# Seven half-depth products for the second MLP matrix, six unit starts moved ahead, and per-head decays in the SSD scan of a hybrid decoder layer

## The chip, the cores and the metric

The kernel runs on one core of a Trainium2 chip. The metric is the device time of one launch in microseconds (us). The kernel before takes 2730.93 us (median of three runs, 2730.6 to 2733.95).

A core has five engines, each with its own queue of instructions taken strictly in order: TensorE (PE; its weight loads are listed as PEld), VectorE (DVE), ScalarE (ACT), GpSimd (POOL) and SyncE (SP, which here only starts DMAs). PE writes into PSUM, eight banks of 128 x 512 float32. A DMA is started by a queue (SP, ACT or POOL) and lands later; what reads its data waits on a semaphore.

## The reference, cut to what matters

The layer maps 1024 tokens of width 1024 (16 meta tokens lead) to the same shape, in float32:

```
h    = rmsnorm(x);  proj = h @ w_in                    # one wide projection
y_a, y_b, y_c = GLA(proj), sliding-window attention(proj), SSD(proj)
x    = x + (g0*(y_a@Wa) + g1*(y_b@Wb) + g2*(y_c@Wc)) @ w_out
h2   = rmsnorm(x)
hid  = square(relu(h2 @ w_mlp_in))                     # 1024 -> 4096
x    = x + hid @ w_mlp_out                             # 4096 -> 1024
out  = rmsnorm(x, final_norm)
# SSD, per head, in chunks of 128 positions:
seg[l,s] = a_cs[l] - a_cs[s];  L = exp(seg) for s <= l, else 0
y = ((C B^T) * L) @ (x*dt) + (C @ S_prev) * exp(a_cs) + D*x
```

## The kernel before, in words

Precision: a float32 operand is split into a high part (a cast to the reduced type `float32r`, on ACT) and a low part (the difference, on DVE). A product is the sum of three matmuls, high x high, high x low and low x high, summed in one PSUM bank. `w_split` and `w_cols` (L118 to L149) make the parts `w_hi` (L127) and `w_lo` (L128) of weights in tiles of 128 x 2048, two of each; `o_split` (L151 to L153) makes those of activations.

The work goes through these stages: normalisation and transposes, the GLA heads, the window attention, four SSD groups (`ssd`, L557), the three branch products with their gates (`branch`), the output projection (`wout`), and the MLP.

SSD scan (L628 to L673, at raised priority): a group has eight chunks. A chunk loads `ab`, the decay sums of its eight heads copied to all partitions (L632, 512 KB, two buffers); POOL subtracts the row's own sum (L635), DVE clips at zero (L636), ACT takes the exponential (L637), DVE multiplies by C B^T (L638), and PE forms eight 64-wide products with it (L643). PE then does C times the state (L646) and the state's update (L657). The sum `y` is gated, normalised (ACT, L664 and L666) and transposed on PE (L669) for the store. Between these steps PE works on "fillers": columns of the projection that do not depend on the scan (`zgen`, `ggen`), which end in L186 to L188 and L158 to L160.

First MLP product (L899 to L1032): a scheme of seven products instead of eight for 2 x 2 blocks (tokens in two halves, depth in two halves). Its activation operands `X` are 28 tiles (`x11`, `x21`, `x22`, `t1` to `t4`), made from transposed `h2` by DVE and ACT just before (L1002 to L1024). The weights come in 16 units of 256 columns; a unit makes four sums on DVE (L913 to L916) and seven operand pairs (L924, L925), and does seven products of 12 matmuls (`prod`, L929 to L937; the matmuls are L933, L935 and L936). Products share PSUM banks by accumulating. Results go through relu and square and to DRAM (`hid_out`, L939).

Second MLP product (L1034 to L1080): sixteen plain blocks of depth 256. A block loads its hidden rows and weights, splits them, and does 16 products of six matmuls of 128 x 512 (`tm2`, L843 to L849); each is added to the result tile `x2b` by DVE (L1062). The last block also does the final normalisation per token tile.

What sets the order: the kernel is written in program order, and a scheduler that models the engines' times at build time lays out one fixed list per engine, with raised priority for the SSD scan. Pools of buffers decide when a load may start.

Of the kernel before, what the change touches and what calls it, by code (L numbers as in the profile page):

```python
# [16 lines left out]
P = 128  # L17
D = 1024
# [26 lines left out]
def hybrid_layer_kernel(ctx, tc, x, meta_tokens, norm_mix, w_in, b_gate, gla_w_gate_up, gla_b_gate_up,  # L45
# [67 lines left out]
    hid_d = [dram.tile([P, SEQ], F32, name=f"hid{i}") for i in range(32)]  # L113

# [3 lines left out]
    def w_split(loads, cols, scales=None):  # L118
        hi = wp.tile([P, 2048], F32R, tag="whi", name="w_hi")
        lo = wp.tile([P, 2048], F32R, tag="wlo", name="w_lo")  # L120
        h = cols // 2
        for i in range(2):
            raw = raw_tile()
            loads(raw[:, :h], i)
            c = slice(i * h, (i + 1) * h)
            if scales is None:
                nc.scalar.copy(hi[:, c], raw[:, :h])  # L127
                nc.vector.tensor_tensor(lo[:, c], raw[:, :h], hi[:, c].bitcast(F32), sub)  # L128
                continue
            n = cols // len(scales)  # L130
            for k in range(h // n):
                sc, rc, c = scales[i * (h // n) + k], slice(k * n, (k + 1) * n), slice(i * h + k * n, i * h + (k + 1) * n)
                nc.scalar.activation(hi[:, c], raw[:, rc], AF.Copy, scale=sc)
                nc.vector.scalar_tensor_tensor(out=lo[:, c], in0=raw[:, rc], scalar=sc, in1=hi[:, c].bitcast(F32),
                                               op0=mult, op1=sub)
        return hi, lo

    def w_cols(view, ranges, scales=None):
        tot = sum(n for _, n in ranges)

        def loads(raw, i):
            rv = raw.rearrange("p (k c) -> p k c", k=KD // 2)
            o = 0
            for c, n in ranges:
                nc.sync.dma_start(rv[:, :, o:o + n], view[:, i * (KD // 2):(i + 1) * (KD // 2), c:c + n])
                o += n
        hi, lo = w_split(loads, KD * tot, scales)
        return (hi[:, :KD * tot].rearrange("p (k c) -> p k c", k=KD),
                lo[:, :KD * tot].rearrange("p (k c) -> p k c", k=KD))  # L149
# [16 lines left out]
    with p1:  # L166
# [390 lines left out]
        def ssd(g):  # L557
# [68 lines left out]
            if g < 3:  # L626
                zfill(8 * FZ[g], g + 1)
            with tc.high_priority(offset=HPE):  # L628
                for c in range(NT):
# [5 lines left out]
                    nc.gpsimd.tensor_tensor(ab, ab, up(tms[:, c, 32 + 8 * g:40 + 8 * g], 2, [P, 8, P]), sub)  # L635
                    nc.vector.tensor_scalar(ab, ab, 0.0, None, op0=amin)  # L636
# [5 lines left out]
                    for h in range(8):  # L642
                        nc.tensor.matmul(psD[:, h * 64:(h + 1) * 64], lhsT=ab[:, h, :], rhs=xd[:, h * 64:(h + 1) * 64],  # L643
                                         start=True, stop=True)
# [22 lines left out]
                    ps = bank(bk, "tr", 2)  # L667
# [444 lines left out]
```

## Time and profile before

| | us |
|---|---|
| median of three runs | 2730.93 |
| the profiled execution, whole | 2735.99 |
| its span in the profile | 2734.4 |
| PE busy in the span | 2634.5 (96%) |
| DVE busy | 1451.0 (53%) |
| ACT busy | 1049.2 (38%) |
| POOL busy | 386.2 (14%) |

The profiled execution is 5.06 us above the median of the runs; 1.59 us of it lie outside the span. Matmuls are pipelined, so their durations overlap: what one costs in a stream is the distance between two starts, not its listed duration. "Idle before" is the time that an engine waited ahead of an instruction and what ended it. The granted clock (PEclk) is a share of TensorE's full speed; it has two levels, 2.4 GHz (1.00) and 1.2 GHz (0.50), and a stretch shows the mean.

### The profile page before, as it was taken

What the parts mean: (1) busy time and instruction counts of PE and PEld (TensorE: products, weight loads), DVE (VectorE), ACT (ScalarE), POOL (GpSimd) and SP (SyncE); (2) the same over time, 40 slices, a digit from 0 to 9 for tenths busy, and PEclk for the clock granted to TensorE, in tenths of its full rate; (3) what the DMA queues carried; (4) which work ended last, traced back from release to release, by engine and by line L of the source; (5) the groups of instructions that cost most, each with busy time, mean ns of one, the idle gap of its engine ahead of it and who ended that gap; (6) DMA issues with size and microseconds to landing.
All of it is one profiled execution on the core that took longest, in us unless ns stands there. A gap on an engine that the chain in (4) does not pass through costs nothing.

```text
span 2734.4 us, 36866 instructions
## 1 busy us (share of the span) xinstructions
PE 2634.5 (96%) x14565; PEld 2284.4 (84%) x14565; DVE 1451.0 (53%) x2463; ACT 1049.2 (38%) x1915; POOL 386.2 (14%) x326
## 2 busy tenths in 40 slices
PE   8999999999999989989989899999998999999998
PEld 7998988888888979879879678888996888888887
DVE  5333323256664573653655653444437666676666
ACT  6423433246664454353454343323234333321212
POOL 1000000011221150340340410322200000000001
PEclk9999999999999999989989999999998999999999
DMA  4211112212223152252251464433322333533231
GB/s 141 63 40 54 47 47 62 77 52 76 61 68 93 51 123 74 67 122 74 76 133 46 122 224 150 150 113 110 124 78 81 108 108 113 204 124 96 93 100 62
DMA packets 223951, 260.48 MB, mean 95 GB/s; under 512 B 14382, under 2 KB 176484, under 8 KB 223780
## 3 DMA queue, kind: packets, MB, share of 16 engines
q1 hardware_dynamic: 178820, 207.74, 25.7%
q10 hardware_dynamic: 44960, 50.40, 5.2%
q8 instruction: 114, 1.87, 0.3%
q14 instruction: 57, 0.47, 0.1%
HBM read 195.05 MB, written 63.05 MB: 94 GB/s over the span
## 4 chain that ended last, share of the span: by engine, by line
PE 80%; DVE 5%; DMA 5%; ACT 4%; issue 3%; POOL 2%; SPq 0%; ACTq 0%; POOLq 0%; DVEq 0%
PE acc_ps L158 8%; PE acc_ps L159 8%; PE acc_ps L160 8%; PE pp_ps L778 8%; PE pp_ps L849 5%; PE pp_ps L847 5%; PE pp_ps L848 5%; PE pp_ps L781 4%; DMA ab<-acs_d 4%; PE pp_ps L933 3%; PE pp_ps L935 3%; PE pp_ps L936 3%; PE acc_ps L186 3%; PE acc_ps L188 3%; PE acc_ps L187 3%
## 5 line engine op out<-in xcount | busy, mean ns | idle before, releaser
L158 PE MATMUL acc_ps<-hh,w_hi 128*128 128x512 f32 (+6 forms) x1320 | 472.0, 358 | 3.3 <-ACT rt L352 1.7
L159 PE MATMUL acc_ps<-hl,w_hi 128*128 128x512 f32 (+6 forms) x1320 | 475.1, 360 | 0.0
L160 PE MATMUL acc_ps<-hh,w_lo 128*128 128x512 f32 (+6 forms) x1320 | 470.6, 356 | 0.0
L186 PE MATMUL acc_ps<-w_hi,hh 128*128 128x256 f32 x1056 | 308.4, 292 | 1.9 <-ACT zst L199 1.3
L187 PE MATMUL acc_ps<-w_lo,hh 128*128 128x256 f32 x1056 | 309.0, 293 | 0.0
L188 PE MATMUL acc_ps<-w_hi,hl 128*128 128x256 f32 x1056 | 308.1, 293 | 0.0
L128 DVE TENSOR_TENSOR w_lo<-w_raw,w_hi 128x1024 fp32r<-128x1024 f32 (+1 forms) x156 | 200.5, 1307 | 155.4 <-ACT w_hi L127 155.3
L158 PEld LDWEIGHTS acc_ps<-hh,w_hi 128*128 128x128 f32 (+1 forms) x1320 | 247.6, 188 | 32.8 <-ACT rt L352 2.6
L847 PE MATMUL pp_ps<-w_hi,o 128*128 128x512 f32 (+1 forms) x768 | 270.7, 354 | 1.4 <-ACT w_hi L127 1.4
L849 PE MATMUL pp_ps<-w_hi,o 128*128 128x512 f32 (+1 forms) x768 | 271.5, 354 | 0.1
L848 PE MATMUL pp_ps<-w_lo,o 128*128 128x512 f32 (+1 forms) x768 | 271.4, 354 | 0.0
L159 PEld LDWEIGHTS acc_ps<-hl,w_hi 128*128 128x128 f32 (+1 forms) x1320 | 247.8, 188 | 26.6 <-issue 2.4
L160 PEld LDWEIGHTS acc_ps<-hh,w_lo 128*128 128x128 f32 (+1 forms) x1320 | 248.0, 188 | 26.0 <-issue 2.4
L127 ACT CAST w_hi<-w_raw 128x1024 fp32r<-128x1024 f32 (+1 forms) x156 | 154.7, 1040 | 274.7 <-PE pp_ps L849 122.2
L188 PEld LDWEIGHTS acc_ps<-w_hi,hl 128*128 128x128 f32 x1056 | 201.3, 191 | 11.2 <-issue 10.5
L186 PEld LDWEIGHTS acc_ps<-w_hi,hh 128*128 128x128 f32 x1056 | 201.6, 191 | 9.2 <-issue 4.7
L187 PEld LDWEIGHTS acc_ps<-w_lo,hh 128*128 128x128 f32 x1056 | 201.3, 191 | 5.3 <-issue 4.4
L781 PE MATMUL pp_ps<-o,w_hi 128*128 128x512 f32 x512 | 198.9, 389 | 0.0
L778 PE MATMUL pp_ps<-o,w_hi 128*128 128x512 f32 x512 | 197.1, 389 | 1.2 <-ACT o L152 1.2
L1062 DVE TENSOR_TENSOR x2b<-pp_ps,x2b 128x512 f32<-128x512 f32 x256 | 169.3, 685 | 45.4 <-PE pp_ps L849 43.5
L933 PE MATMUL pp_ps<-o,w_hi 128*128 128x512 f32 x448 | 177.4, 398 | 9.3 <-ACT o L152 9.2
L935 PE MATMUL pp_ps<-o,w_hi 128*128 128x512 f32 x448 | 177.2, 395 | 2.1 <-DVE o L153 2.1
(298 smaller groups left out, 4657.1 us busy)
## 6 DMA issues: line engine op xcount, KB each, us to landing
w_raw<-in_w_in_dram SPq DMA_DIRECT2D x80, 512.0 KB, 3.7
ab<-acs_d SPq DMA_DIRECT2D x32, 512.0 KB, 9.2
g<-gate SPq DMA_DIRECT2D x64, 256.0 KB, 4.0
w_raw<-in_w_mlp_in_dram SPq DMA_DIRECT2D x32, 512.0 KB, 4.1
hid<-hid ACTq DMA_DIRECT2D x64, 256.0 KB, 3.3
w_raw<-hid SPq DMA_DIRECT2D x32, 512.0 KB, 4.4
w_raw<-in_w_mlp_out_dram SPq DMA_DIRECT2D x32, 512.0 KB
gate<-gst ACTq DMA_DIRECT2D x48, 256.0 KB, 2.0
```

Of the source, the lines that this page charges most:

```text
L158: nc.tensor.matmul(ps, lhsT=lh, rhs=rh, start=(i == 0), stop=False)
L159: nc.tensor.matmul(ps, lhsT=lh, rhs=rl, start=False, stop=False)
L160: nc.tensor.matmul(ps, lhsT=ll, rhs=rh, start=False, stop=(i == n - 1))
L186: nc.tensor.matmul(o, lhsT=h_h, rhs=whi[:, k, off:off + width], start=(k == 0), stop=False)
L187: nc.tensor.matmul(o, lhsT=h_h, rhs=wlo[:, k, off:off + width], start=False, stop=False)
L188: nc.tensor.matmul(o, lhsT=h_l, rhs=whi[:, k, off:off + width], start=False, stop=(k == KD - 1))
L778: nc.tensor.matmul(ps[b], lhsT=lh, rhs=xs[b][:, 0, :], start=(st and k == 0), stop=(sp_ and k == n - 1))
L781: nc.tensor.matmul(ps[b], lhsT=lh, rhs=xs[b][:, 1, :], start=False, stop=False)
L847: nc.tensor.matmul(ps, lhsT=x[:, 0], rhs=rh, start=(i == 0), stop=False)
L848: nc.tensor.matmul(ps, lhsT=x[:, 0], rhs=rl, start=False, stop=False)
L849: nc.tensor.matmul(ps, lhsT=x[:, 1], rhs=rh, start=False, stop=(i == n - 1))
L933: nc.tensor.matmul(ps, lhsT=h[:, kk, :], rhs=x[:, 0, :], start=(first and kk == 0), stop=False, skip_group_check=True)
```

## The change

1. The second MLP product is done in seven half-depth products too. The hidden units are taken in four groups (`q`) of eight units; a group does seven products, each 4 token tiles x 4 depth steps x 3 matmuls of 128 x 512. The activation operands (`x11`, `x21`, `x22`, `t1` to `t4`) are written by the first product's units: `t1` to `t4` are sums that POOL forms there, so a unit now stores seven tiles where it stored four. The weight operands `s1` to `s4` are sums that POOL forms in place. Results are added to tiles of `x2b` and to a fourth set `rr`, which the last group adds to three quarters of the result.
2. In the first MLP product each product has its own PSUM bank, and DVE combines them afterwards.
3. The products `x11` and `x21` of units 0 to 5 are done early, two units at a time, between the steps that make the operands (`pre`). Their intermediate result goes to DRAM and comes back by a DMA on POOL's queue; so does the finished `x11` tile.
4. In the SSD scan the subtraction and the clipping of the decays become eight DVE instructions, one for each head, with the head's sum as a per-partition scalar. The transposes of a chunk's `y` are issued after the next chunk's eight products.
5. Weight parts lie in tiles of 128 x 1024, four of each instead of two of double width; `final_norm` is loaded late; the final normalisation is done as the quarters of the last group finish.

The diff, cut to its core:

```diff
-        hi = wp.tile([P, 2048], F32R, tag="whi", name="w_hi")
-        lo = wp.tile([P, 2048], F32R, tag="wlo", name="w_lo")
+    def hilo():
+        return (wp.tile([P, 1024], F32R, tag="whi", name="w_hi", bufs=4),
+                wp.tile([P, 1024], F32R, tag="wlo", name="w_lo", bufs=4))
...
-                    nc.gpsimd.tensor_tensor(ab, ab, up(tms[:, c, 32 + 8 * g:40 + 8 * g], 2, [P, 8, P]), sub)
-                    nc.vector.tensor_scalar(ab, ab, 0.0, None, op0=amin)
+                    for h in range(8):
+                        nc.vector.tensor_scalar(ab[:, h, :], ab[:, h, :], tms[:, c, 32 + 8 * g + h:33 + 8 * g + h], 0.0,
+                                                op0=sub, op1=amin)
...
+                    if c:
+                        with tc.issue_after(mm.ins):
+                            y_out(c - 1, yn)
...
+        def pre(u):
+            ws_ = []
+            for i in range(2):
+                raw = raw_tile()
...
+                hi, lo = hilo()
+                nc.scalar.copy(hi, raw)
+                nc.vector.tensor_tensor(lo, raw, hi.bitcast(F32), sub)
...
+            for v in range(2):
+                w = [[t[:, :, v * P:(v + 1) * P] for t in pair] for pair in ws_]
+                a = ps_tile()
+                prod(a, w[0], "x11", True, True)
+                p1 = g_tile()
+                nc.scalar.copy(p1, a)
+                nc.scalar.dma_start(p1_d[u + v], p1)
+                unit_b(u + v, {"a": a, "w": {2: w[1]}})
...
+            if u < NPRE:
+                nc.gpsimd.dma_start(st["p1"], p1_d[u])
+                return
...
-            prod(st["b"], st["w"][7], "t3", False, True)
-            nc.vector.tensor_tensor(st["u3"], st["b"], st["p1"], sub)
+            b = ps_tile()
+            prod(b, st["w"][7], "t3", True, True)
+            nc.vector.tensor_tensor(st["u3"], b, st["u2"], add)
...
+            nc.gpsimd.tensor_tensor(t1, st["x11"], g, sub)
+            hid_out(u, "t1", t1)
+            nc.gpsimd.tensor_tensor(t2, st["x22"], t1, add)
+            hid_out(u, "t2", t2)
+            nc.gpsimd.tensor_tensor(t3, g, st["x22"], sub)
+            hid_out(u, "t3", t3)
+            nc.gpsimd.tensor_tensor(t4, st["x21"], t2, sub)
+            hid_out(u, "t4", t4)
...
-        NB = 16
-        for blk in range(NB):
...
+        def product(ps, xo, wo, first, last, done):
+            for t in range(4):
+                ts = slice(t * P, (t + 1) * P)
+                for kk in range(4):
+                    (xh, xl), (wh, wl) = xo[kk], wo[kk]
...
+                done(t, ps[t])
...
+        for q in range(NQ):
...
+            product(a, *o1, True, True, first_r)
+            product(a, *o2, False, True, evict("c11", add))
+            b = four()
+            product(b, x_op(q, "t3"), w_op(q, wr, "s3"), True, True, evict("c22", add))
+            a = four()
+            product(a, x_op(q, "t2"), w_op(q, wr, "s2"), True, True, evict("r", sub))
...
+            product(b, x_op(q, "t4"), w_op(q, wr, "a22"), False, True, c21_done)
+            c = four()
...
+            product(c, x_op(q, "t1"), w_op(q, wr, "s1"), True, True, c22_done)
+            product(c, x_op(q, "x22"), w_op(q, wr, "s4"), False, True, c12_done)
```

Three places in the engines' lists are shown. On PE, in a scan chunk before, the transposes of `y` (L669) stand ahead of the next chunk's eight products (L643), with filler matmuls (`acc_ps`) in front of them:

```order
L187 MATMUL acc_ps<-w_lo,hh_172 128x256
L188 MATMUL acc_ps<-w_hi,hl_180 128x256
L186 MATMUL acc_ps<-w_hi,hh_173 128x256
L669 MATMUL ps_tr<-ident,y 128x128 x4
L643 MATMUL ps_y<-xd,ab 128x64 x8
L646 MATMUL ps_y<-S,CF 128x512
L657 MATMUL ps_y<-xe,BT 128x512
L187 MATMUL acc_ps<-w_lo,hh_173 128x256
```

In the changed kernel the same eight products are L666, C times the state is L672, the state's update is L683 and the transposes are L644:

```order
L201 MATMUL acc_ps<-w_hi,hl_214 128x256
L666 MATMUL ps_y<-xd,ab 128x64 x8
L672 MATMUL ps_y<-S,CF 128x512
L199 MATMUL acc_ps<-w_hi,hh_199 128x256
L200 MATMUL acc_ps<-w_lo,hh_199 128x256
L201 MATMUL acc_ps<-w_hi,hl_207 128x256
L199 MATMUL acc_ps<-w_hi,hh_200 128x256
L644 MATMUL ps_tr<-ident,y 128x128 x4
L683 MATMUL ps_y<-xe,BT 128x512
```

The transposes of a chunk moved from ahead of the next chunk's products to behind them, beside the state matmuls.

On PE at the start of the MLP, before: the transposes of `h2` (L892) of the second token half with the matmuls of unit 0 (L933, L935, L936) between them:

```order
L892 MATMUL pp_ps<-ident,h_17706 128x128 x7
L892 MATMUL pp_ps<-ident,h_17715 128x128 x7
L933 MATMUL pp_ps<-o,w_hi 128x512
L892 MATMUL pp_ps<-ident,h_17724 128x128 x7
L935 MATMUL pp_ps<-o,w_hi 128x512
L936 MATMUL pp_ps<-o,w_lo 128x512
L933 MATMUL pp_ps<-o,w_hi 128x512
L935 MATMUL pp_ps<-o,w_hi 128x512
L936 MATMUL pp_ps<-o,w_lo 128x512
L892 MATMUL pp_ps<-ident,h_17733 128x128 x7
```

The same place now, where the matmuls L954, L956 and L957 belong to the early products of units 0 to 5 and L905 are the transposes:

```order
L905 MATMUL pp_ps<-ident,h_18066 128x128 x2
L905 MATMUL pp_ps<-ident,h_18075 128x128 x4
L905 MATMUL pp_ps<-ident,h_18084 128x128 x4
L954 MATMUL pp_ps<-o,w_hi 128x512 x4
L905 MATMUL pp_ps<-ident,h_18093 128x128 x4
L956 MATMUL pp_ps<-o,w_hi 128x512
L957 MATMUL pp_ps<-o,w_lo 128x512
L954 MATMUL pp_ps<-o,w_hi 128x512
L956 MATMUL pp_ps<-o,w_hi 128x512
L957 MATMUL pp_ps<-o,w_lo 128x512
```

From the first transpose of `h2` to the last matmul of the early products PE's list now holds 64 transposes and 180 matmuls of 512 columns; the early products are 144 of them.

On DVE in the second MLP product, before: additions to the result (L1062) with the low parts of the next block's weights (L128) and hidden rows (L153):

```order
L128 TENSOR_TENSOR w_lo<-w_raw,w_hi 128x1024
L1062 TENSOR_TENSOR x2b_20046<-pp_ps,x2b_20046 128x512
L1062 TENSOR_TENSOR x2b_20048<-pp_ps,x2b_20048 128x512 x2
L1062 TENSOR_TENSOR x2b_20050<-pp_ps,x2b_20050 128x512
L153 TENSOR_TENSOR o<-w_raw,o 128x512
L1062 TENSOR_TENSOR x2b_20050<-pp_ps,x2b_20050 128x512
L153 TENSOR_TENSOR o<-w_raw,o 128x512
L1062 TENSOR_TENSOR x2b_20052<-pp_ps,x2b_20052 128x512 x2
```

Now, with the additions at L1212, low parts of weights at L1192 and of hidden rows at L1161:

```order
L1212 TENSOR_TENSOR x2b_20704<-x2b_20704,pp_ps 128x512
L1192 TENSOR_TENSOR w_lo<-o,w_hi 128x1024
L1212 TENSOR_TENSOR x2b_20705<-x2b_20705,pp_ps 128x512
L1161 TENSOR_TENSOR o<-raw_21506,o 128x1024
L1192 TENSOR_TENSOR w_lo<-o,w_hi 128x1024
L1212 TENSOR_TENSOR o<-o,pp_ps 128x512 x3
L1161 TENSOR_TENSOR o<-raw_21512,o 128x1024
L1212 TENSOR_TENSOR o<-o,pp_ps 128x512
```

A product of 48 matmuls now has four additions and four low parts of 1024 columns around it; the low parts of later operands stand between the additions of the product that is running.

## Rows read from the trace of the kernel before

**Rows 1.** Page, part 1: busy time, share and instructions of each engine.
```profile
PE 2634.5 (96%) x14565; PEld 2284.4 (84%) x14565; DVE 1451.0 (53%) x2463; ACT 1049.2 (38%) x1915; POOL 386.2 (14%) x326
```

**Rows 2.** Busy time by stretch: us, each engine's busy time (count), PEclk, DMA share, GB/s.
```profile
103.00:500.00 397.00, 394.68 (x2597) 353.32 (x2596) 122.33 (x246) 136.65 (x255) 22.61 (x34) 1.00 0.16 49
850.00:1598.00 748.00, 693.92 (x4259) 627.43 (x4258) 421.13 (x585) 318.50 (x495) 200.72 (x152) 0.95 0.34 89
...
2037.55:2080.00 42.45, 28.36 (x114) 18.91 (x112) 36.79 (x63) 33.63 (x61) 5.07 (x4) 0.73 0.13 44
2080.00:2708.00 628.00, 626.64 (x2761) 518.62 (x2762) 415.25 (x633) 156.43 (x251) 0.09 (x1) 1.00 0.33 110
```

**Rows 3.** Busy time by stretch: the four SSD scans.
```profile
954.00:1038.00 84.00, 70.32 (x458) 60.39 (x457) 56.09 (x70) 43.88 (x63) 42.05 (x33) 0.92 0.51 122
1134.00:1225.00 91.00, 77.54 (x425) 63.09 (x424) 55.15 (x70) 39.37 (x58) 45.09 (x33) 0.87 0.49 112
1335.00:1420.00 85.00, 72.20 (x452) 61.26 (x451) 54.93 (x70) 43.39 (x62) 42.22 (x33) 0.88 0.51 121
1515.00:1597.00 82.00, 72.85 (x356) 55.41 (x355) 54.96 (x69) 29.92 (x49) 37.75 (x31) 0.96 0.41 113
```

**Rows 4.** Waits of PE, 850 to 1600 us: total us, times, longest.
```profile
PE ps_tr L669 <- ACT y L666: 39.3, 20, 4.9
PE ps_y L643 <- DVE ab L638: 11.0, 8, 2.7
```

**Rows 5.** Timeline: start, us, engine, line; three of PE's matmuls and 32 transposes.
```profile
2037.55 3.66 PE L892 MATMUL pp_ps<-ident,h 128*128 128x128 f32 x32
...
2695.74 0.39 PE L847 MATMUL pp_ps<-w_hi,o 128*128 128x512 f32 x1
...
2708.66 0.39 PE L847 MATMUL pp_ps<-w_hi,o 128*128 128x512 f32 x1
...
2724.08 0.39 PE L849 MATMUL pp_ps<-w_hi,o 128*128 128x512 f32 x1
```

**Rows 6.** DVE groups by form: count, busy us, mean ns, idle before and releaser.
```profile
L128 DVE TENSOR_TENSOR w_lo<-w_raw,w_hi 128x1024 fp32r<-128x1024 f32 x154 | 199.7, 1319 | 155.4 <-ACT w_hi L127 155.3
L1062 DVE TENSOR_TENSOR x2b<-pp_ps,x2b 128x512 f32<-128x512 f32 x256 | 169.3, 685 | 45.4 <-PE pp_ps L849 43.5 <-PE pp_ps L936 1.5
L638 DVE TENSOR_TENSOR ab<-ab,cb 128x1024 f32<-128x1024 f32 x32 | 43.3, 1363 | 13.0 <-ACT ab L637 13.0
L636 DVE TENSOR_SCALAR ab<-ab 128x1024 f32<-128x1024 f32 x32 | 35.6, 1112 | 85.1 <-POOL ab L635 85.1
L872 DVE TENSOR_SCALAR h<-x,rs 128x1024 f32<-128x1024 f32 x8 | 6.0, 750 | 2.5 <-POOL rs L88 2.5
L532 DVE TENSOR_SCALAR mxs<-mxs 128x4 f32<-128x4 f32 x32 | 7.6, 238 | 0.7
L86 DVE TENSOR_SCALAR ms<-yss 128x1 f32<-128x1 f32 x32 | 4.7, 148 | 15.1 <-ACT zt L664 14.9
```

**Rows 7.** ACT groups by form.
```profile
L127 ACT CAST w_hi<-w_raw 128x1024 fp32r<-128x1024 f32 x154 | 154.0, 1048 | 274.7 <-PE pp_ps L849 122.2 <-PE acc_ps L159 72.0 <-PE pp_ps L781 63.8
L924 ACT CAST w_hi<-mt 128x512 fp32r<-128x512 f32 x64 | 39.6, 622 | 102.9 <-PE pp_ps L935 57.4 <-DVE mt L913 45.0 <-DVE mt L914 0.4
L637 ACT ACTIVATE ab<-ab 128x1024 f32<-128x1024 f32 x32 | 33.8, 1057 | 42.6 <-DVE ab L636 42.5
```

**Rows 8.** POOL groups by form.
```profile
L635 POOL TENSOR_TENSOR ab<-ab,tms 128x1024 f32<-128x1024 f32 x32 | 63.4, 1980 | 139.9 <-DMA ab<-acs_d 127.6 <-PE acc_ps L188 8.5 <-PE ps_y L657 3.7
```

**Rows 9.** Timeline, 1835 to 1844 us: POOL additions and DVE side by side.
```profile
1835.70 5.43 POOL L817 TENSOR_TENSOR mg<-mg,g 128x512 f32<-128x512 f32 x4 [16.34 <-DVE g L816]
...
1837.49 5.90 DVE L134 SCALAR_TENSOR_TENSOR w_lo<-w_raw,vecs,w_hi 128x256 fp32r<-128x256 f32 x8
```

**Rows 10.** The line L134: shortest, median and longest duration in ns.
```profile
L134 DVE SCALAR_TENSOR_TENSOR w_lo<-w_raw,vecs,w_hi x64: 468/474/1519, 1750.5 to 1908.2; 128x256 fp32r<-128x256 f32 x64
```

**Rows 11.** Page, part 6: DMA issues, KB each, median us to landing.
```profile
ab<-acs_d SPq DMA_DIRECT2D x32, 512.0 KB, 9.2
g<-gate SPq DMA_DIRECT2D x64, 256.0 KB, 4.0
```

More of the change, by code (lines that the diff above doesn't have):

```diff
@@ L627, in ssd, with y_out @@
                 zfill(8 * FZ[g], g + 1)
+            def y_out(c, y):
+                ps = bank(bk, "tr", 2)
+                for i in range(4):
+                    nc.tensor.transpose(out=ps[:, i * P:(i + 1) * P], in_=y[:, i * P:(i + 1) * P], identity=ident)
+                st = ep.tile([P, CH], F32, tag="st", name="yst", bufs=2)
+                nc.scalar.copy(st, ps)
+                nc.scalar.dma_start(ossd[g].rearrange("(i p) t -> p i t", p=P)[:, :, c * P:(c + 1) * P],
+                                    st.rearrange("p (i t) -> p i t", i=4))
             with tc.high_priority(offset=HPE):
@@ L666, in ssd @@
                     nc.scalar.activation(y, y, AF.Copy, scale=rs)
[L667 to L673 removed]
+                    yn = y
+                y_out(NT - 1, yn)
         es = ExitStack()
@@ new lines, in hybrid_layer_kernel, with final, final_out @@
+        ys, sqs = {}, {}
+        def final(t, n):
+            if t not in sqs:
+                sqs[t] = sm.tile([P, 2], F32, tag="sq", name="sq", bufs=8)
+            y = tp.tile([P, 512], F32, tag="g", name="ysq", bufs=4)
+            nc.scalar.activation(y, x2[t][:, n * 512:(n + 1) * 512], AF.Square, accum_out=sqs[t][:, n:n + 1])
+        def final_out(t):
+            ss = sm.tile([P, 1], F32, tag="ss", name="ss3")
+            nc.vector.tensor_tensor(ss, sqs[t][:, 0:1], sqs[t][:, 1:2], add)
+            rs = rstd_of(ss, D, "rs3")
+            for n in range(2):
+                c = slice(n * 512, (n + 1) * 512)
+                y = x2[t][:, c]
+                if t < NT - 1 and n == 1:
+                    nc.scalar.activation(y, y, AF.Copy, scale=rs)
+                    nc.gpsimd.tensor_tensor(y, y, fnb[:, c], mult)
+                else:
+                    nc.vector.scalar_tensor_tensor(out=y, in0=y, scalar=rs, in1=fnb[:, c], op0=mult, op1=mult)
+                nc.sync.dma_start(out2d[t * P:(t + 1) * P, c], y)
@@ new lines, in hybrid_layer_kernel, with x_op @@
+        acc_c = {"c11": [], "c21": [], "c12": [], "c22": []}
+        for t in range(NT):
+            b = t // 4
+            acc_c["c12" if b else "c11"].append(x2[t][:, 0:512])
+            acc_c["c22" if b else "c21"].append(x2[t][:, 512:1024])
+        rr = []
+        for i in range(2):
+            t = hl_tile().bitcast(F32)
+            rr += [t[:, 0, :], t[:, 1, :]]
+        acc_c["r"] = rr
+        NQ, fnb = 4, None
+        def x_op(q, nm):
+            tiles = []
+            for i in range(2):
+                if q == 0 and nm in ("x11", "x21"):
+                    r = raw_tile().rearrange("p (v t) -> p v t", v=2)
+                else:
+                    r = tp.tile([P, 2, 512], F32, tag="h2", name="raw2", bufs=4)
+                nc.sync.dma_start(r, hid_d[2 * q + i, nm].rearrange("(v p) t -> p v t", p=P))
+                hi, lo = hl_tile(), hl_tile()
+                nc.scalar.copy(hi, r)
+                nc.vector.tensor_tensor(lo, r, hi.bitcast(F32), sub)
+                for v in range(2):
+                    tiles.append((hi[:, v, :], lo[:, v, :]))
+            return tiles
```

278 lines of the change are left out of this document (169 added, 109 removed).

## The prediction

> **What bounds the kernel now.** I began with the page's busy times [rows 1]: PE is busy for 96% of the span, so time goes only where PE gets less work or where it waits or runs slow today. The table by stretch says where that is [rows 2]. The GLA stretch is full (394.7 of 397 us), and so is the MLP from 2080 us (626.6 of 628, granted clock 1.00). Two places are not full. The SSD part has PE busy for 694 of 748 us, and the MLP's first 42 us have PE busy for 28, at a mean clock of 0.73. Third came the four scans [rows 3]: 342 us in all, PE busy for 293, so 49 us idle, with a clock of 0.87 to 0.96; the lost share of the clock times each length is another 32 us. The waits there [rows 4] say that PE stood 20 times in front of the transposes of `y` (39.3 us) and 8 times in front of the products with `ab` (11.0). The tail is fourth: the last matmul starts at 2724.08 [rows 5] and the span is 2734.4, so about 10 us are left for the last additions and the normalisation.
>
> **A. Second product, fewer matmuls.** Before: 16 blocks x 16 products x 6 = 1536 matmuls of 512 columns. Now: 4 groups x 7 products x 48 = 1344, so 192 are gone. In the full stretch one costs 626.64/2761 = 0.227 us [rows 2]; two starts 57 matmuls apart, 12.92 us [rows 5], say the same. PE sets the pace there, so 192 x 0.227 = **-43.6 us**. What has to be hidden beside a product of 48 x 0.227 = 10.9 us: DVE has four low parts of 1.32 and four additions of 0.685, 8.0 us [rows 6]; ACT four casts of 1.05, 4.2 us [rows 7]; POOL two sums of 1.98 [rows 8] in four of seven products. Each fits. Low parts rise from 64 to 112 of 1024 columns, additions to the result fall from 256 to 124, which for DVE is a gain of 27 us off the path.
>
> **B. Start of the MLP.** The stretch 2037.55 to 2080 holds 64 transposes at 3.66/32 = 0.114 us [rows 5] and 50 matmuls at 0.227: 18.7 us of work at full speed in 42.45, so 23.7 are lost to waits for operands and to the low clock. The list now holds 64 transposes and 180 matmuls there, 48.2 us. ACT has its 33.6 us [rows 2] and six casts of 1.05, and a net thirteen operations of 512 columns at 0.62 [rows 7]: 48 us. DVE has 36.8 and six low parts of 1.32 less two sums of 0.685: 43.3. PE and ACT are then level, so I take 52 us, 3.8 lost: **-19.9 us**. If nothing is lost it is -23.7; if the three engines hand work over as badly as today and the stretch takes 64 us, -8.
>
> **C. Units 0 to 5.** They now have five products left, 60 x 0.227 = 13.6 us. DVE has 18 operations of 512 columns (four sums, five low parts, nine combinations, each product now being its own bank) at 0.685 [rows 6]: 12.3 us. POOL adds beside it: four POOL additions of that size, 5.43 us, ran beside eight DVE operations that took 5.90 [rows 9], where a median one of them takes 0.474 [rows 10], so 3.8: 2.1 us more. That makes 14.4 against 13.6, 0.8 x 6 = 5 us. The new waits add to it. The twelve reloads of `p1` and `x11` are started from POOL's queue, behind its additions; DVE's subtraction waits for `p1` with all later combinations queued behind it, and POOL's `t1` waits for `x11`, with three more sums and the next reload behind it. A load half as large lands 4.0 us after its issue, and at the worst 9.2 [rows 11]; a unit lasts 14, so most are early, and I put 3 us for six units. **+8 us**, from 0 to 25. In units 6 to 15 DVE has 20 x 0.685 + 2.1 = 15.8 against 84 x 0.227 = 19.1: hidden.
>
> **D, E, F. Smaller terms.** The second product's first operands become free only as the last unit ends, and `x2b` is loaded again: **+4** (0 to 12, the far end being one landing [rows 11] and one cast and low part). Steady contention of POOL's sums with DVE over 28 products: **+3** (0 to 20, the far end by rival 3). The tail: the normalisation now starts as quarters finish, about two fewer DVE passes at the end: **-2** (-4 to +2).
>
> The finer weight tiles of edit 5 have the same count and size of casts; GLA, where most of them are, is full: 0 (-3 to +3). The MLP's sum is -50.5, from -73 to -24.
>
> **G. The scans.** A scan's chunk takes 342/32 = 10.7 us. Its `ab` has two buffers, so one loop of load, use and release may take two periods. Before, the loop is: landing 9.2 [rows 11], POOL's subtraction 1.98 [rows 8], clip 1.11, exponential 1.06 [rows 7], multiplication 1.36 [rows 6], and 16 PE starts at the 0.114 of [rows 5], 1.9: 16.6 us, with hand-overs about 18, that is 8.9 us a chunk at least. POOL's idle time before L635 ends mostly on that load (127.6 of 139.9 us) [rows 8], so POOL itself is not what is late. Now POOL's step is gone, and the clip becomes eight operations of 128 columns. No such form is in the trace; it lies between 0.148 for one column and 0.238 for four, which is a small operation's fixed part, and 0.750 for 1024 columns [rows 6]. I take 0.19, 1.5 us for eight; the far end 0.238, 1.9 us. The loop shrinks by 1.98 - 0.4 = 1.6 to 1.7, 0.85 a chunk, 27 us over 32 chunks if the loop sets the pace. To it I add 9 us, a quarter of the 39.3 that PE stood in front of the transposes [rows 4]: behind the products they no longer hold back the next chunk, but the state's update L683 and the fillers still stand behind them. **-36 us.** The two ends: PE's own work in the scans at full clock is 293 less the clock's part, about 265, 8.3 a chunk; if that sets the pace at 8.4, the gain is 2.3 x 32 = 73. If DVE sets the pace (221/32 = 6.9 us a chunk now [rows 3]) and the eight operations cost 0.238 each, 0.8 x 32 = 25 us are added.
>
> **The sum.** -43.6 - 19.9 + 8 + 4 + 3 - 2 - 36 = -86.5. The profiled execution is 2735.99 us (a span of 2734.4 and 1.59 around it), so a like execution takes 2649.5. The median of the runs is 5.06 below the profiled one, which gives 2644.4, said as **2645 us**.
>
> **Rivals.**
> 1. The scans gain nothing: the load of `ab` sets their pace and DVE's extra work eats POOL's step. For it: the 127.6 us [rows 8]. Against it: the step does leave the loop. 2645 + 36 = 2681.
> 2. The scans become PE's, and the MLP has no new stalls: 37 us more there, and 13 of C, D and E not paid. For it: PE's 39.3 us of waits in its own queue [rows 4]. 2595.
> 3. POOL's additions hold DVE for their whole time. For units 0 to 5 DVE then has 12.3 + 5.43 = 17.8 against 13.6, 4.2 x 6 = 25 us; in the 16 products with sums 8.0 + 3.96 = 12.0 against 10.9, 18 us. Against 8 us allowed for these two, 35 more: 2680. For it: DVE's eight operations stretched beside POOL [rows 9]; against it: by 2.1 us and not by 5.43.
>
> The Trainium skill bears on this rival (SBUF — State Buffer, "SBUF: two separate sides"): DVE, in an operation with two SBUF inputs, and GpSimd hold a shared pair of ports as an exclusive lock for a whole instruction, and the other "fully blocks". By that rule the time is rival 3's; the trace agrees in the direction and shows 2.1 of 5.43 us.
>
> 4. Slower than before: the second product's operands are late at each of its 28 products. There are four weight tiles of each part, two products' worth. From a freed tile to the next operand stand two casts of 1.05, two low parts and two splits of hidden rows of 1.32, and four additions of 0.685 queued between them, 10.1 us in 10.9. With POOL's two sums in the same chain it is 14.1, 3.2 late, and with 0.3 for hand-overs 3.5 x 28 = 98 us: 2743. It decides from 86/28 = 3.1 us late per product. Against it: only 16 products have such sums, they can be formed ahead, and a landing of 4 to 9 us is ahead of the tile.
>
> That the change doesn't do what it says I leave out: the engines' lists show the transposes behind the products, and 144 early matmuls.
>
> **How the numbers follow.** Forecast 0.57, own range 2612 to 2680 (the ends of B to F and a third of G's); rival 1 0.14, rival 2 0.12, rival 3 0.12, rival 4 0.05. The range of 8 in 10 is 2600 to 2695: it takes in rivals 1 and 3, both with some ten us on top, and leaves out rival 4 and about half of rival 2. A measurement of this kernel tells 0.2%, some 5.5 us, from no change. Only rival 4 ends above: slower 0.05, the same 0.02 (from its edge), faster 0.93.
>
> **What would show it.** A: 1344 matmuls at 0.227 us in the second product, PE gapless; an average above 0.24 is E or rival 4, and PE's waits would name L1192 or POOL's L1183. B: from the first transpose of `h2` to the last early product some 52 us, clock near 1. C: 14.5 us a unit, waits at the subtraction of `p1`. G: scans near 76 us instead of 85, the wait of the transposes on `y` mostly gone, DVE's eight operations under 0.2 us each; 85 us again is rival 1, 67 rival 2. Rival 3: DVE's 512-column operations lasting over 1 us beside POOL. It is wrong altogether if PE is idle for over 80 us in the second product.

## The result and the profile after

The changed kernel takes 2697.99 us, median of four runs (2695.72 to 2701.56), beside 2730.76 us for the kernel before on the same chip: a ratio of 0.9879, 95% interval 0.9862 to 0.9896. The forecast was 2645 us with a range up to 2695. The profiled execution took 2697.15 us with a span of 2695.5. The spans differ by 38.9 us and the medians by 32.8, since the profiled execution of before lay 5 us above its median and this one did not.

Busy times of the changed kernel [rows 1], page, part 1:

```profile
PE 2612.5 (97%) x14373; PEld 2245.8 (83%) x14373; DVE 1502.5 (56%) x2577; ACT 1096.4 (41%) x1930; POOL 513.9 (19%) x402
```

Its stretches [rows 2] in the same columns (us, busy time and count of PE, PEld, DVE, ACT, POOL, then PEclk, DMA share, GB/s). In order: GLA, the SSD stage from 850 us to the first branch matmul, the branches, the start of the MLP to the last transpose of `h2`, a part of the first product, the start and the rest of the second:

```profile
103.00:500.00 397.00, 395.16 (x2594) 354.00 (x2594) 126.58 (x249) 137.99 (x257) 22.60 (x34) 1.00 0.17 51
...
850.00:1591.30 741.30, 689.55 (x4228) 620.44 (x4226) 425.27 (x806) 322.35 (x497) 134.62 (x120) 0.95 0.34 90
1591.30:1949.00 357.70, 357.68 (x1534) 288.00 (x1535) 150.57 (x210) 121.30 (x213) 62.09 (x45) 1.00 0.42 142
2041.60:2074.60 33.00, 30.79 (x164) 24.73 (x163) 27.74 (x45) 28.26 (x50) 3.75 (x5) 1.00 0.40 128
...
2100.00:2300.00 200.00, 200.00 (x860) 161.18 (x859) 162.03 (x220) 53.30 (x93) 76.44 (x54) 1.00 0.51 170
...
2365.70:2450.00 84.30, 79.43 (x327) 63.11 (x326) 62.55 (x54) 30.83 (x34) 28.93 (x12) 0.96 0.69 240
2450.00:2687.00 237.00, 237.00 (x1021) 191.97 (x1019) 183.50 (x193) 88.87 (x112) 77.35 (x36) 1.00 0.37 123
```

The same two stages of the kernel before, SSD and branches, cut at their own ends:

```profile
850.00:1595.30 745.30, 691.22 (x4248) 625.29 (x4246) 419.07 (x583) 315.88 (x492) 200.72 (x152) 0.95 0.34 90
1595.30:1944.80 349.50, 348.30 (x1537) 288.09 (x1536) 153.13 (x210) 121.39 (x215) 64.83 (x45) 1.00 0.44 146
```

Two things stand out. The SSD stage, where 36 us were to be won, became only 4 us shorter, with 20 fewer matmul starts in it: PE is idle for 52 us as for 54 before, at the same clock. And the branches, whose matmuls did not change, take 8 us more with PE full in both. Cut to 300 us inside that stage, before and after:

```profile
1620.00:1920.00 300.00, 300.00 (x1325) 248.50 (x1324) 132.55 (x186) 101.63 (x185) 57.49 (x40) 1.00 0.42 137
```
```profile
1620.00:1920.00 300.00, 300.00 (x1288) 241.45 (x1287) 124.26 (x175) 96.98 (x176) 55.53 (x40) 1.00 0.38 127
```

PE starts 1325 matmuls in 300 us before and 1288 after: 0.2264 and 0.2329 us each, the clock at 1.00 in both. A part of the first product (200/860 = 0.2326) and the rest of the second (237/1021 = 0.2321) run at the slower pace too. Over the 4224 matmuls of 512 columns from the branches on, 6 ns each are an estimated 25 us that no step of the prediction had.

In the scans the waits have moved [rows 4]. Waits of the changed kernel, 850 to 1600 us (total us, times, longest):

```profile
DVE ab L658 <- DMA ab<-acs_d: 98.6, 27, 9.9
...
PE ps_tr L644 <- ACT y L692: 15.2, 10, 4.5
...
PE ps_y L666 <- DVE y L677: 8.6, 4, 3.4
...
PE ps_y L666 <- DVE ms L86: 7.5, 5, 2.7
...
PE ps_y L666 <- DVE ab L661: 6.6, 2, 3.4
PE ps_y L672 <- DVE S L686: 5.6, 3, 2.6
```

Before, the wait for the load of `ab` stood on POOL (127.6 us, rows 8), which also has steps of `y` and of the state behind it, but is busy for only 201 of the stage's 745 us. Now it is in DVE's list, with 425 us of work. What that does in one chunk is in the timeline of the changed kernel:

```profile
1162.27 0.47 SPq L654 DMA_DIRECT2D ab<-acs_d  x1
...
1169.26 0.19 ACT L690 ACTIVATION_READ_ACCUMULATOR zt<-y 128x1 f32 x1
...
1172.20 1.66 DVE L658 TENSOR_SCALAR ab<-ab,tms 128x128 f32<-128x128 f32 x8 [3.56 <-DMA ab<-acs_d]
...
1173.78 1.22 DVE L144 TENSOR_TENSOR w_lo<-w_raw,w_hi 128x1024 fp32r<-128x1024 f32 x1
...
1174.91 0.14 DVE L86 TENSOR_SCALAR ms<-yss 128x1 f32<-128x1 f32 x1
1174.98 0.67 DVE L677 TENSOR_TENSOR y<-y,ps_y 128x512 f32<-128x512 f32 x1
...
1175.72 0.72 ACT L692 ACTIVATE y<-y,yrs 128x512 f32<-128x512 f32 x1 [0.77 <-POOL yrs L88]
...
1176.49 0.66 PE L644 MATMUL ps_tr<-ident,y 128*128 128x128 f32 x4 [3.41 <-ACT y L692]
...
1177.26 0.41 PE L200 MATMUL acc_ps<-w_lo,hh 128*128 128x256 f32 x1
```

DVE starts on the load 9.9 us after its issue and has stood 3.56 us in front of it. The row's sum of squares was ready at 1169.45, but `ms` (L86) and the next sum of `y` (L677) stand behind the eight operations and a low part (L144), and run at 1174.9. So ACT scales `y` late and PE idles 3.41 us. Its matmuls then come some 0.2 us apart in place of 0.12: the granted clock of 1176.4 to 1178.0 us is 0.74.

The same can be counted over all four scans. Each of PE's waits between 930 and 1592 us was followed back from its end, over at most 12 us, through what released each step. Of 50 us of idle time in the changed kernel, 41 go back to DVE's wait for `ab`; of 50 in the kernel before, 28 go back to POOL's.

### The profile page after: what moved, and what is told of

Same layout as the page of the kernel before. It is cut to its first block, busy times and chain, and to the rows that moved or that the text cites. A ratio compares the mean times of both kernels' runs of the same rounds, so it can differ in the third digit from the quotient of the medians.

```text
span 2695.5 us, 36835 instructions
## 1 busy us (share of the span) xinstructions
PE 2612.5 (97%) x14373; PEld 2245.8 (83%) x14373; DVE 1502.5 (56%) x2577; ACT 1096.4 (41%) x1930; POOL 513.9 (19%) x402
## 4 chain that ended last, share of the span: by engine, by line
PE 83%; DMA 8%; DVE 4%; ACT 3%; issue 2%; POOL 0%; SPq 0%; ACTq 0%; DVEq 0%; POOLq 0%
PE pp_ps L798 9%; PE acc_ps L171 9%; PE acc_ps L172 9%; PE acc_ps L173 8%; DMA ab<-acs_d 6%; PE pp_ps L801 4%; PE pp_ps L1204 4%; PE pp_ps L1205 4%; PE pp_ps L1202 3%; PE pp_ps L954 3%; PE pp_ps L957 3%; PE pp_ps L956 3%; PE acc_ps L199 3%; PE acc_ps L201 3%; PE acc_ps L200 3%
## 5 line engine op out<-in xcount | busy, mean ns | idle before, releaser
L144 DVE TENSOR_TENSOR w_lo<-w_raw,w_hi 128x1024 fp32r<-128x1024 f32 (+1 forms) x124 | 156.9, 1267 | 204.4 <-ACT w_hi L143 201.1
L143 ACT CAST w_hi<-w_raw 128x1024 fp32r<-128x1024 f32 (+1 forms) x124 | 128.4, 1036 | 206.9 <-PE acc_ps L172 86.7
L1204 PE MATMUL pp_ps<-w_lo,o 128*128 128x512 f32 x448 | 178.5, 399 | 3.7 <-DVE w_lo L1192 3.7
L1205 PE MATMUL pp_ps<-w_hi,o 128*128 128x512 f32 x448 | 178.2, 398 | 0.0
L1202 PE MATMUL pp_ps<-w_hi,o 128*128 128x512 f32 x448 | 176.1, 397 | 1.2 <-ACT w_hi L1191 1.2
L954 PE MATMUL pp_ps<-o,w_hi 128*128 128x512 f32 x448 | 176.1, 396 | 1.1 <-ACT o L165 0.8
L956 PE MATMUL pp_ps<-o,w_hi 128*128 128x512 f32 x448 | 177.1, 395 | 0.0
L957 PE MATMUL pp_ps<-o,w_lo 128*128 128x512 f32 x448 | 176.3, 395 | 0.0
```

The source lines that it names most:

```text
L956: nc.tensor.matmul(ps, lhsT=h[:, kk, :], rhs=x[:, 1, :], start=False, stop=False, skip_group_check=True)
L957: nc.tensor.matmul(ps, lhsT=l[:, kk, :], rhs=x[:, 0, :], start=False, stop=(last and kk == 3), skip_group_check=True)
L1204: nc.tensor.matmul(ps[t], lhsT=xh[:, ts], rhs=wl, start=False, stop=False, skip_group_check=True)
L1205: nc.tensor.matmul(ps[t], lhsT=xl[:, ts], rhs=wh, start=False, stop=(last and kk == 3), skip_group_check=True)
```

## The experiments

**Placement of tiles.** The final normalisation asks for eight buffers of the 8-byte tile `sq` where there were four. A buffer takes 32 bytes in the pool, so every tile allocated behind it lies 128 bytes further. In the built program the weight parts `w_hi`, `w_lo` lie at 96 modulo 256 in both kernels; the activation parts `o` lay at 96 and now lie at 224.

`e1_pad`, 128 bytes more, all engines' lists unchanged:

```diff
-                sqs[t] = sm.tile([P, 2], F32, tag="sq", name="sq", bufs=8)
+                sqs[t] = sm.tile([P, 2], F32, tag="sq", name="sq", bufs=12)
```

> Theory P (placement): in the changed kernel the four more buffers of the 8-byte tile sq move every tile behind them by 128 bytes, so the moving and the stationary operands of the 512-column matmuls no longer lie a multiple of 256 bytes apart; that costs 5 to 6 ns on each of the 4224 such matmuls from the branches on. Four further buffers of sq bring the distance back to a multiple of 256 and change no instruction. P expects 0.227 us a matmul again in the branch stage and the second product, 342 us for the branch stage instead of 350, and 23 to 26 us off the whole: about 2674 us. Rival N (neighbours): the matmuls are slower because DVE, POOL and the DMAs are busier beside them; then nothing changes: 2698 us, 0.233 us.

2675.49 us, ratio 0.9783 (0.9768 to 0.9797) to before. The same 300 us of its branches:

```profile
1620.00:1920.00 300.00, 300.00 (x1325) 248.43 (x1324) 127.34 (x180) 98.68 (x178) 55.43 (x40) 1.00 0.40 132
```

`e2_before_shifted`, the opposite edit in the kernel before (lists unchanged):

```diff
-                            sq = sm.tile([P, 2], F32, tag="sq", name="sq")
+                            sq = sm.tile([P, 2], F32, tag="sq", name="sq", bufs=8)
```

> The kernel before with eight buffers of sq instead of four: all that stands behind is moved by 128 bytes, no instruction changes. Theory P: 4416 matmuls of 512 columns at 0.2325 instead of 0.227 us, 24 to 26 us slower than before, about 2756 us. Rival N: the same time as before, 2731 us.

2761.12 us beside 2735.08, ratio 1.0094 (1.0076 to 1.0112): 26 us slower. Its branches:

```profile
1620.00:1920.00 300.00, 300.00 (x1288) 241.57 (x1287) 132.21 (x186) 100.70 (x183) 57.56 (x40) 1.00 0.41 135
```

`e10_both_shifted`, e1 with 128 bytes ahead of the weights as well, so that weights and activations are at 224 both:

```diff
+    gap = ctx.enter_context(tc.tile_pool(name="gap", bufs=1)).tile([P, 32], F32, name="gap")
+    nc.gpsimd.memset(gap, 0.0)
     wp = ctx.enter_context(tc.tile_pool(name="wp", bufs=2))
```

> e1 with 128 bytes put ahead of the weight tiles, so that the weight tiles and the activation tiles behind them both move by 128 bytes and stay a multiple of 256 apart. If the distance of a matmul's two operands counts, a 512-column matmul stays at 0.227 us and the whole within 4 us of e1. If the place of the activation tiles itself counts (it is now that of the changed kernel), it is 0.2325 us and 23 to 26 us slower than e1.

2673.44 us, ratio 0.9776 (0.9760 to 0.9792): fast again. Its branches:

```profile
1620.00:1920.00 300.00, 300.00 (x1326) 248.39 (x1325) 127.97 (x181) 98.68 (x178) 57.63 (x42) 1.00 0.39 130
```

The second product of e1 has the faster pace again (200/884 = 0.2262 us):

```profile
2450.00:2650.00 200.00, 200.00 (x884) 165.66 (x883) 159.69 (x167) 74.67 (x89) 63.87 (x26) 1.00 0.40 128
```

So what counts is where the two operands lie relative to each other, not the place of one, and N (busier neighbours) falls: e1 has the changed kernel's lists, and so its neighbours. The runs tried only the distances 0 and 128 modulo 256. The GLA stretch, where the activation tiles lie at four places, adds to this: with the built program's addresses laid beside the trace of before, 512-column matmuls there follow each other after 0.2325 to 0.2328 us at distances of 64, 128 and 192, and after 0.2305 at 0. The sign is the same and the size a third; why 0 is not as fast there stays open. Matmuls of 256 columns behind the branches show no difference (0.120 us at 0 and at 128).

**The scans.** The kernels below start from e1 (2675 us). For each, the stage from 850 us to its first branch matmul. Each edit but that of e4 makes the scheduler lay out PE's and DVE's lists anew, so the order of fillers moves along with it.

| | stage, us | PE idle in it | PEclk | whole |
|---|---|---|---|---|
| before | 745.3 | 54.1 | 0.95 | 2731 to 2735 |
| e1 | 744.3 | 52.9 | 0.94 | 2675.49 |
| e3, decay on POOL | 751.4 | 56.9 | 0.94 | 2683.79 |
| e4, the same lists as e1 | 741.8 | 47.1 | 0.94 | 2673.63 |
| e5, three `ab` | 736.9 | 48.4 | 0.94 | 2668.51 |
| e8, and loads ahead | 731.2 | 48.3 | 0.96 | 2666.79 |
| e9, `ab` loaded once | 694.1 | 24.7 | 0.98 | 2623.20 |
| e11, e8 with `ab` behind `y` | 682.1 | 21.9 | 0.99 | 2612.64 |
| e12, e1 with `ab` behind `y` | 718.1 | 47.0 | 0.95 | 2652.95 |

`e3_decay_on_pool`:

```diff
-                    for h in range(8):
-                        nc.vector.tensor_scalar(ab[:, h, :], ...
+                    nc.gpsimd.tensor_tensor(ab, ab, up(tms[:, c, 32 + 8 * g:40 + 8 * g], 2, [P, 8, P]), sub)
+                    nc.vector.tensor_scalar(ab, ab, 0.0, None, op0=amin)
```

> e1 with the old decay: POOL subtracts the sums, DVE clips; the transposes stay behind the next products. Theory D (DVE takes over the waiting): the per-head operations put the wait for the load of ab (98.6 us in 27 waits) into DVE's queue, and the steps of y behind it are late; what the shorter loop gains is lost there. D expects the scans within 6 us of e1 in sum, the wait for ab back on POOL, and PE's waits in front of the products smaller. Rival L (loop): the load, POOL's step and the rest set the pace and the removed step was worth its 0.85 us a chunk; then this is about 27 us slower than e1, and something else made up for it in the changed kernel.

Ratio 0.9820 (0.9800 to 0.9840), 8 us above e1. The products' first-to-last distances sum to 283.3 us, e1's to 279.8: D's 6 us hold by this measure, L's 27 do not. The stage is 7.1 us longer, so the per-head decay is worth some 7 to 8 us, between the two and nearer to D. POOL waits for `ab` again (147.3 us), and PE in front of the transposes (40.1 us), which stand where they stood in the kernel before although the deferral is still in the code. With the same decay and the same place of the transposes, its stage is still 6.1 us longer than that of before; what costs this is not shown, but it is why the decay's gain is hardly seen in the result.

`e4_transposes_first`:

```diff
-                    if c:
-                        with tc.issue_after(mm.ins):
-                            y_out(c - 1, yn)
...
-                    yn = y
-                y_out(NT - 1, yn)
+                    y_out(c, y)
```

> e1 with the transposes of y issued at the end of their own chunk again, as before; the decay stays per head. If the deferral is worth what the prediction gave it, this is 9 us slower than e1; if the deferral only moved PE's wait from the transposes to the products, it is within 4 us of e1, with PE waiting some 39 us in front of the transposes and under 10 in front of the products.

2673.63 us, ratio 0.9776 (0.9756 to 0.9795). But the edit changes nothing that is built: all five engines' lists, with operands and waits, are those of e1. So this is e1 a second time, and its waits (12.9 us in front of the transposes, some 21 in front of the products) are e1's own (14.6 and some 24). It shows how far two runs of one program lie apart: 1.9 us in the median, 2.5 in the stage, 5.8 in PE's idle time.

The lists say why. The deferral asks that the transposes of a chunk stand behind the next chunk's products, and in the kernel before they did already: those that stand ahead of a chunk's products are of two chunks earlier. (The description of the change takes them for those of the chunk before, which is wrong.) With the old decay, too, the lists are the same with and without the deferral. It is the per-head decay that moved the transposes, in half of the scans behind one chunk's products more, and with it PE's wait in front of them went from 40.1 us (e3) to 14.6 (e1).

`e5_three_ab`:

```diff
-                    ab = ep.tile([P, 8, P], F32, tag="ab", name="ab", bufs=2)
+                    ab = ep.tile([P, 8, P], F32, tag="ab", name="ab", bufs=3)
```

> e1 with three buffers of ab instead of two (and one of yst instead of two, for room). In e1 DVE stands in front of a landing of ab for 84.7 us in 25 waits. Theory W (the wait for the load, now in DVE's queue, sets the scan's pace): with the load a chunk earlier these waits shrink to under 30 us, the products' first-to-last distance falls from 280 us in the four scans to 240 to 255, and the whole is 25 to 40 us faster than e1: about 2640 us. Rival Y (the chain of y and the state, or SP's queue in front of the load, sets it): DVE's wait shrinks or moves, the scans stay within 6 us of 280, the whole within 6 us of e1's 2675.

Ratio 0.9760 (0.9745 to 0.9774), 7 us better than e1; the four scans take 266.9 us. Between both expectations: DVE still waits 69 us for `ab` in the scans (from 930 us on; e1 84.7). Its list took up the operations earlier too: those of chunk 3 now stand ahead of chunk 0's last step of `y`, where e1 has those of chunk 2.

`e8_ab_ahead`:

```diff
-                    nc.sync.dma_start(ab, acs_d[8 * g:8 * g + 8, c * P:(c + 1) * P].partition_broadcast(P))
+                    ab = abs_.pop(c)
+                    if c < NT - 1:
+                        ab_load(c + 1)
                     zt = ep.tile([P, CH], F32, tag="zt", name="zt", bufs=2)
```

> e5 with the load of ab for the next chunk placed on SP's queue ahead of this chunk's load of zt, which waits for the square of two chunks ago (137 us of SP's waits in e1). Theory W: if the third buffer alone is eaten by SP's wait in front of zt, this one shows the gain: scans at 240 to 255 us, about 2640 us. If e5 has it already, this adds under 6 us. Rival Y: both stay at 2675.

Ratio 0.9753 (0.9738 to 0.9767): within 2 us of e5, whose lists of PE, DVE and POOL it has, and DVE waits 66.9 us still. An earlier load alone is not it.

`e9_ab_loaded_once` (28 of 32 loads left out, so that its result is not the layer's):

```diff
-                    nc.sync.dma_start(ab, acs_d[8 * g:8 * g + 8, c * P:(c + 1) * P].partition_broadcast(P))
+                    if c == 0:
+                        ab0 = ep.tile([P, 8, P], F32, tag="ab0", name="ab0", bufs=1)
+                        nc.sync.dma_start(ab0, acs_d[...].partition_broadcast(P))
...
-                        nc.vector.tensor_scalar(ab[:, h, :], ab[:, h, :], ...
+                        nc.vector.tensor_scalar(ab[:, h, :], ab0[:, h, :], ...
```

> e1 with ab loaded once a group instead of once a chunk: every chunk's eight per-head operations read that one tile, so chunk 0's sums serve all chunks, and 28 of 32 loads are left out. DVE never stands in front of a landing within a group. Theory W2 (DVE's in-order wait for the landing, 84.7 us in e1 and still 67 with three buffers, holds back the steps of y behind it and so PE): the products' first-to-last distance falls from 280 us to 235 to 250. Rival Y (the chain of y, DVE's own work and the low clock set it): it stays at 262 or more, about what the third buffer brought.

2623.20 us, ratio 0.9591 (0.9576 to 0.9605), scans 245.9 us: W2. Y falls, since the chain of `y` and DVE's own work are all still there. Of 24 us that PE still idles from 930 us on, 1 goes back to a wait for `ab`.

`e11_ab_after_y`, on e8, with nothing left out (`ymul` holds the multiplication of `y` by `zt` of each chunk):

```diff
+                    with tc.issue_after(ymul[c - 2]) if c > 1 else ExitStack():
                         for h in range(8):
                             nc.vector.tensor_scalar(ab[:, h, :], ab[:, h, :], ...
```

> e8 with the eight per-head operations of a chunk placed in DVE's list behind the last step of y of two chunks earlier, when the load has landed. Nothing is left out. W2: DVE's wait for ab falls from 67 us to under 20 and the scans from 264 to 240 to 252, the whole to 2640 to 2655 us. Rival Y: the wait falls, the scans stay within 5 us of 264, the whole within 5 us of e8's 2667.

2612.64 us, ratio 0.9552 (0.9538 to 0.9566). Its stage and its DVE waits in it:

```profile
850.00:1532.10 682.10, 660.20 (x4240) 601.96 (x4238) 438.91 (x807) 317.85 (x494) 145.16 (x120) 0.99 0.38 98
```
```profile
DVE ab L667 <- DMA ab<-acs_d: 26.4, 6, 9.2
```

The wait for `ab` is 26 us, 13.5 of them from 930 us on, inside the scans (251.8 us, as W2 said). PE's idle time falls by 31 us from e1's, and its busy time, for as many matmuls, by another 31: the granted clock rose from 0.94 to 0.99. That second half is why the whole is better than W2 said.

`e12_wait_behind_y`, on e1:

```diff
+                    with tc.issue_after(ymul[c - 1]) if c else ExitStack():
                         for h in range(8):
```

> e1 (two buffers, loads as in the changed kernel) with one edit: a chunk's eight per-head operations stand in DVE's list behind the last step of y of the chunk before. The load is not earlier, so DVE still waits for it, but no step of y stands behind that wait. Theory W2: the scans shrink from 280 us to 250 to 268, PE's idle time in the SSD stage from 52 to under 40, the whole to 2630 to 2660 us. Rival E (only an earlier load helps, as in e9 and e11): DVE waits for ab as in e1 (85 us) and the whole stays within 6 us of e1's 2675.

2652.95 us, ratio 0.9703 (0.9691 to 0.9716): 22 us off e1 with two buffers and no load earlier, and DVE's wait for `ab` is nonetheless down to 23.4 us in 4 waits. The whole is as W2 said, two of its signs are not: PE idles 47 us, as in e4, and the scans are longer, 384 us first to last. The scheduler laid out PE's list anew: in the first three scans 49 to 85 filler matmuls stand between two chunks' products where e1 has 14 to 40, and in the last scan they run out. Up to its last scan e12 takes 609.8 us for 3883 matmul starts, e1 659.5 for 3882; the last scan with what follows in the stage takes 108.3 us in e12 and 84.8 in e1. So this run does not part the order of DVE's list from that of the fillers; for W2 it is e9 and e11 that count most, where the lists move less. A scan's length is a poor measure here; the stage is the one to read. PE's waits in it are now nearly one:

```profile
PE ps_y L669 <- DVE ab L664: 36.3, 9, 6.9
```

**The MLP.** `e6_no_early_units`, on e1:

```diff
-    NPRE = 6
+    NPRE = 0
```

> e1 without early products (no unit is begun ahead, nothing is reloaded on POOL's queue). If the early products are what fills the start of the MLP, the first product from the first transpose of h2 to its last matmul takes 20 to 26 us more than e1's 316, and the whole is about 2698 us. Rival: if the separate banks bring the gain, or the reloads cost what the early products bring, it is within 6 us of e1.

2688.40 us, ratio 0.9828 (0.9809 to 0.9848). The first product takes 328.9 us from its first transpose to its last matmul, e1's 316.1, that of before 344.0, where 25 matmuls of the second product (5.7 us) already run inside that time. So the early products are worth 13 us, half of what was expected; some 9 more come with the rest of the new unit scheme, which this run does not take apart.

`e7_x2b_later`, on e1 (the loads of `x2b` in halves, each behind the operand loads of a product):

```diff
-                for t in range(NT):
-                    nc.sync.dma_start(x2[t], x2_d[t * P:(t + 1) * P, :])
...
+            x2_load(range(4), 0)
             product(a, *o1, True, True, first_r)
+            o3 = x_op(q, "t3"), w_op(q, wr, "s3")
+            x2_load(range(4, 8), 1)
             product(a, *o2, False, True, evict("c11", add))
```

> e1 with the loads of x2b split into halves and each issued behind the operand loads of the product before its use. In e1 the second and third product of the second MLP matrix lose 9.9 us to three waits and to the low clock behind them, while the DMA engines are full with the 4 MB of x2b (393 GB/s). If those loads hold up the operands, 6 to 9 us go: about 2668 us. Rival: if the operands are late because their tiles come free late and POOL's sums are in the chain, it is within 2 us of e1.

2676.10 us, ratio 0.9787 (0.9773 to 0.9802): nothing. The loads of `x2b` are not what holds up the second and third product. Whether it is the freed tiles or POOL's sums no run takes apart, but the trace shows POOL's sums in the longest of these waits. In the changed kernel:

```profile
2397.33 3.34 POOL L1183 TENSOR_TENSOR o<-o,w_raw 128x1024 f32<-128x1024 f32 x1
...
2398.38 3.38 DVE L1192 TENSOR_TENSOR w_lo<-o,w_hi 128x1024 fp32r<-128x1024 f32 x1
...
2401.82 0.50 PE L1204 MATMUL pp_ps<-w_lo,o 128*128 128x512 f32 x1 [2.56 <-DVE w_lo L1192]
```

The low part takes 3.38 us beside POOL's sum, and 1.22 us (median of 39) where it runs without POOL; PE waits 2.56 us for it.

## Why the prediction was wrong

The direction was right and the range missed by 3 us. That it missed by so little is in part luck: two errors of 25 to 32 us were offset in part by costs that did not come. By its own terms, from the spans:

- **A**, right: 192 matmuls fewer, and with the placement mended (e1) the second product runs at 0.2262 us (884 starts in 200 us), PE gapless but for its start. After that start DVE's and POOL's work is hidden, as said. In the changed kernel itself a matmul costs 0.2321 us and not the 0.227 of the sum.
- **B**, right: the first 33.0 us hold 64 transposes and 100 matmuls, 30.0 us of work, at clock 1.00; 3.0 us are lost where 3.8 were forecast and 23.7 were lost before. To the 180th matmul it is 52.7 us (52 forecast), against 72.9 before; without the early products (e6) it is 64.8, e1 52.0, so 13 of these 20 us are theirs.
- **C**, +8 forecast, 0 measured: from 2100 to 2300 us PE has no gap; DVE is busy for 162 of 200 us.
- **D**, +4 forecast: 327 matmuls in the first 84.3 us at 0.2321 are 75.9, so 8.4 are lost, inside the 0 to 12 that was given. **E**, +3 forecast, 0 after that start, where PE has no gap. **F**, -2 forecast, -1.6 measured: the last matmul starts at 2686.8 of 2695.5, so the tail is 8.7 us for 10.3.
- **G**, -36 forecast, -4 measured. This is the step that failed: "27 us over 32 chunks if the loop sets the pace", and 9 more for the transposes. The prediction's own loop asked for 8.9 us a chunk where a chunk took 10.7, so it had not shown the loop to set the pace. The loop did lose POOL's step, but with it the wait for the load went to DVE's list, with the steps of `y` and of the state behind it (98.6 us of waits; 41 of PE's 50 idle us go back to them). By e3 the per-head decay was worth 7 to 8 us and not 27. The 9 us had nothing under them: the deferral changes no engine's list. The prediction asked what stands behind a wait of the reloads in C and not of `ab`. The recoverable time was there (rival 2 had 73 us at most; e11 takes 62 from e1's stage), and it hung on where the eight operations stand. The price taken for one, 0.19 us, was nearly right where eight run in a row (1.66 us); 12 of the 256, beside an operation of POOL, took 0.56 to 1.14 us each. Rival 1 had the size (next to no gain) but not the whole reason: with all loads kept, e11 shows that they do not set the pace in themselves.
- **Not in the sum at all**: 25 us for the 128 bytes that come with edit 5's last part. The prediction set that edit's finer weight tiles at 0, from -3 to +3, and had no term for where tiles lie. e1 gives 22.5 us between medians; its chip ran the kernel before 4.3 us slower, and by the two ratios it is 26.
- Two of its sums do not come out, without weight for the forecast. The far ends of the MLP's terms add up to -74 and +10, not to -73 and -24, and C, D and E in rival 2 to 15, not 13. And of the 5.43 us in [rows 9] only 3.64 lie beside the eight operations of DVE, so "2.1 of 5.43 us" understates how far POOL holds DVE.

Either of the two, G or the placement, put right would have left the time within the range: 2675 with the placement alone, and an estimated 2662 (2698 less the 36) with G as forecast.

On rival 3: DVE's low parts of weights take longer beside POOL's sums, and so do POOL's sums. The means of the changed kernel, over those beside each other and those alone:

```profile
L1192 DVE TENSOR_TENSOR w_lo<-o,w_hi 128x1024 fp32r<-128x1024 f32 x48 | 79.9, 1666 | 10.0 <-ACT w_hi L1191 10.0
```
```profile
L1183 POOL TENSOR_TENSOR o<-o 128x1024 f32<-128x1024 f32 x16 | 44.1, 2764 | 164.4 <-DMA o<-in_w_mlp_out_dram 148.2 <-DVE w_lo L1192 16.2
```

1666 ns in place of 1319 [rows 6], and 2764 in place of 1980 [rows 8]. Taken apart, a low part of L1192 takes 1.22 us without POOL and up to 3.42 beside it, and in the kernel before an operation of L134 takes 0.473 us without POOL and 1.51 (median) beside it. From 2450 us on it costs nothing, since PE stays full; in the first 84 us of the second product PE waits 3.7 us in two waits for such low parts (part of D).

The Trainium skill's rule of an exclusive lock (SBUF — State Buffer, "SBUF: two separate sides") is borne out by the trace: 1.22 us became up to 3.42, which is about the low part and one whole sum of POOL (1.98 [rows 8]). The time of rival 3, 2680 us, did not follow from it, since DVE's idle time took up nearly all of the waiting; the 2698 came from other places.

## What to carry to other kernels

When a step is moved from one engine to another, its wait moves too: ask what stands behind it in the new list, and put the step where its data have landed. Buffers and earlier loads helped little until the list also took the operations up later (7 to 9 us without that, 63 with it). Before pricing a change of order, look whether the built lists differ: the deferral here moved nothing. When an untouched stage changes its pace with the clock at 1.00 in both, compare where its tiles lie: four more buffers of an 8-byte scratch tile cost more here than the scan gained.

## What the runs showed of the hardware

The rate of 512-column matmuls depends on where their moving and stationary tiles lie to each other: at a distance of 0 modulo 256 bytes 1325 starts in 300 us, at 128 1288, in four kernels of both kinds, and with both tiles moved alike 1326 (in the GLA stretch the difference is a third of this). The Trainium skill (SBUF — State Buffer, "Who interferes with whom") says that "only the shared port pair causes contention", the pair of DVE and GpSimd. That sentence is about engines hindering each other; these runs show a second case where a place in SBUF costs time, on TensorE alone, and do not show by what mechanism. A version that beats both kernels is e11: 2612.64 us, 122 us under the kernel before.
